# Two products per key tile in place of three: one key head's values stored as high and low parts side by side, and the halves of the result added

## The chip, the cores and the metric

The kernel runs on one core of one Trainium2 chip. The metric is device time in microseconds (us), the median of several runs. In the profile PE is TensorE (PEld is its weight loads), DVE is VectorE, ACT is ScalarE, POOL is GpSimd and SP is the queue that issues the transfers. A product is written as moving data streamed past a stationary operand (the "weights") that is loaded before.

## The reference, cut to what matters

One step of a one-layer encoder: a recurrent group and a sparse attention group side by side, an output projection, and a gated feed-forward part. There are 1024 new frames of one stream (the prompt) and 8 streams of 16 frames with a cache of 512 (the samples). The change touches the attention of the prompt alone:

```
# 8 query heads of width 64 in two groups of 4; each group shares one of 2 key heads (kv = 0, 1)
s = einsum('bthgd,btkhd->bthgk', q, k[sel]) * 64 ** -0.5     # scores, the keys that were not selected are masked
p = softmax(s)
o = einsum('bthgk,btkhd->bthgd', p, v[sel])                   # values: 64 numbers per key and key head
```

Everything is float32. The kernel keeps that accuracy on TensorE by splitting an operand x into a high part (x rounded to the faster fp32r form) and a low part (x minus the high part), and by adding the products high x high, high x low and low x high.

## The kernel before, in words

The rows of the prompt are cut into 8 tiles of 128 frames, a ninth tile holds the samples. The stages follow each other: normalise and project keys, values and index keys (`norm_kv`); index scores; the recurrent group and the queries, with the search for the selected keys beside them; the first half of the output projection; attention, which runs from about 499 to 672 us of the span and is the stage that the change is in; the second half of the output projection with the second normalisation (`out_tile`); the feed-forward part, more than half of the span.

Each engine runs its instructions in an order fixed beforehand. A planner in the kernel (`run`, line 93) steps through generators, four at a time in attention, by its own estimates of each engine's time; a scheduler behind it then places the instructions by estimates too. `ATT_ORDER` (line 415) names the generators: `attn(i, kv)` for query tile i and key head kv, and `sample_attn(b)` for the eight streams, mixed in between the last prompt tiles.

`attn(i, kv)` (line 1372) goes in three steps. First, for each of its 4 query heads, scores for the (i + 1) * 128 keys allowed (`qk`, two matmuls per piece), then one DVE instruction that masks and finds the maximum (tile m), ACT's exp, and POOL's division by the sum. Then, for each tile kt of 128 keys, `flip` transposes the 4 heads' probabilities (4 transposes of 128x128, line 217 of the profile, into one PSUM bank) and `split` writes their high part with ACT and their low part with DVE into one of four buffers `pT` (in the tiles rest and smr). Last, `product(kt)` (line 1431) multiplies them with the values and gathers all key tiles in one PSUM bank, `po`; after the last one ACT copies the 64 rows that belong to this key head to yF (line 1454).

The values are split once, in `norm_kv` (lines 582 and 583, POOL for the high and DVE for the low part) into `vhl`: for each tile a block of 128 columns of high parts (64 for each key head) and a block of 128 columns of low parts. `mm3` (line 245) issues the three matmuls: low values with high probabilities, high with low, high with high. Their output has 128 rows, and the 64 of the other key head are not used. There are 36 pairs of query tile and key tile and two key heads, so 72 products and 216 matmuls of 512 columns.

The lines of helpers in the profile: L207 is any split matmul, L217 a transpose, L1556 the transposes of the samples' probabilities, L66 every instruction of DVE, ACT and POOL.

Of the kernel before, what the change touches and what calls it, by code (L numbers as in the profile page):

```python
# [14 lines left out]
AF = mybir.ActivationFunctionType  # L15
ALU = mybir.AluOpType
# [6 lines left out]
NP = 8  # L23
# [58 lines left out]
class Kernel:  # L82
# [470 lines left out]
    def norm_kv(self, i, tp, g, wk):  # L553
        nc, I, O = self.nc, self.I, self.O
        self.n_norm += 1
        x = self.x.pop(i, None)
        if x is None:
            x = tp.tile([128, D], F32, tag="x", name="x", bufs=4)
            nc.sync.dma_start(x, self.x_src(i))
        if i < len(self.X_T):  # L560
            yield from self.until(self.X_T[i])
        yield from self.norm_T(x, x, g, self.h[i // 3], (i % 3) * 128, tp)
        t = self.ready
        yield 0.0
        yield from self.until(max(t, self.WK_T))
        pk = self.ps()
        for d in range(ND):
            self.mm3(pk[:, :328], self.h_lhs(i, d, 0), self.h_lhs(i, d, 1), wk[:, d, 0, :], wk[:, d, 1, :],
                     d == 0, d == ND - 1)
        self.begin()  # L570
        kv = tp.tile([128, 328], F32, tag="kv", name="kv")
        nc.scalar.activation(kv, pk[:, :328], AF.Copy)
        tab = self.tables(tp, i)
        kr = tp.tile([128, 64], F32, tag="kr", name="kr")
        self.rope(kr[:, None, :], kv[:, None, 256:320], tab, 1, tp, "dve", self.KR_E[i > 2], "dve")
        t = self.end() + self.KV_LAT
        nc.gpsimd.tensor_scalar(self.kn[:, i, :], kv[:, 0:128], 1.0, 0.0, op0=ALU.mult, op1=ALU.add)
        sq = tp.tile([128, 128], F32, tag="sq", name="sq")
        for a in range(2):
            nc.scalar.activation(sq[:, a * 64:a * 64 + 64], kv[:, a * 64:a * 64 + 64], AF.Square, scale=0.125,  # L580
                                 accum_out=self.kss[:, i, a:a + 1])
        self.hi(self.vhl[:, i, 0, :], kv[:, 128:256], "pool")
        self.lo(self.vhl[:, i, 1, :], kv[:, 128:256], self.vhl[:, i, 0, :])
        vo = O["v_p"][0, i * 128:(i + 1) * 128] if i < NP else O["v_s"].rearrange("b t k d -> (b t) k d")
        nc.sync.dma_start(vo.rearrange("t k d -> t (k d)"), kv[:, 128:256])
        nc.gpsimd.tensor_scalar(self.wi[:, i, :], kv[:, 320:328], 8.0 ** -0.5 * 64.0 ** -0.5, 0.0,
                                op0=ALU.mult, op1=ALU.add)
        ko = O["ki_p"][0, i * 128:(i + 1) * 128] if i < NP else O["ki_s"].rearrange("b t d -> (b t) d")
        nc.sync.dma_start(ko, kr)
        yield 0.0  # L590
        yield from self.until(t)
        self.stack_keys(kr, self.ki1[:, i * 128:(i + 1) * 128], self.ki2[:, i * 128:(i + 1) * 128])
# [779 lines left out]
    def attn(self, i, kv, tp):  # L1372
        nc = self.nc
        W = 128 * (i + 1)
        nch = 1 if W <= 512 else 2
        n = W // nch
        mask = self.mask01[:, 256 - W:] if i < 2 else self.s[i]
        while not self.k_done or i not in self.masked or i not in self.q_ok or (kv and i not in self.qst):
            yield 0.5
        if kv == 0:  # L1380
            self.begin()
            self.qst[i] = self.stack_queries(self.qn[:, i, :], 4, self.raw, "raw")
            self.qst_t[i] = self.end()
            yield 0.0
        yield from self.until(self.qst_t[i])
        qe, qo = self.qst[i]
        pb = []
        per = 2 if nch == 1 else 1
        turn = self.m_next
        self.m_next += 1  # L1390
        for j in range(4):
            h = 4 * kv + j
            if j % per == 0:
                while self.wused >= self.SLOTS or self.m_turn != turn:
                    yield 0.5
                self.wused += 1
                ms = self.wr.tile([128, 1024], F32, tag="w", name="m")
            self.begin()
            m = ms[:, 512 * (j % per):]
            mx = tp.tile([128, 4], F32, tag="mx", name="mx", bufs=6)  # L1400

            for c in range(nch):
                sl = slice(c * n, (c + 1) * n)
                pc = self.ps()
                self.qk(pc[:, :n], qe, qo, h, self.k1[:, kv, sl], self.k2[:, kv, sl])
                nc.vector.tensor_tensor_reduce(m[:, sl], pc[:, :n], mask[:, sl], -0.125, mx[:, 0:1] if c else -LOW,
                                               ALU.add, ALU.min, mx[:, c:c + 1])
            t0 = self.chain
            nc.scalar.activation(m[:, :W], m[:, :W], AF.Exp, scale=-1.0, bias=mx[:, nch - 1:nch],
                                 accum_out=mx[:, 3:4])  # L1410
            nc.vector.reciprocal(mx[:, 3:4], mx[:, 3:4])
            nc.gpsimd.tensor_scalar(m[:, :W], m[:, :W], mx[:, 3:4], 0.0, op0=ALU.mult, op1=ALU.add)
            pb.append(m)
            self.m_turn += j == 3
            t = self.end()
            yield 0.0
            yield from self.until(t if j == 3 else t0 - self.AHEAD)
        po = self.ps()
        pTs, ready = {}, {}

        def flip(kt):
            pt = self.ps()
            for j in range(4):
                self.tr(pt[:, j * 128:(j + 1) * 128], pb[j][:, kt * 128:(kt + 1) * 128])
            x = self.pT_free.pop(0)
            pTs[kt] = (x, x.rearrange("p (x n) -> p x n", x=2))
            self.begin()
            self.split(pTs[kt][1], pt)
            ready[kt] = self.end()

        def product(kt):
            x, pT = pTs.pop(kt)
            self.mm3(po, self.vhl[:, kt, 0, :], self.vhl[:, kt, 1, :], pT[:, 0], pT[:, 1], kt == 0, kt == i)
            self.pT_free.append(x)

        for kt in range(i + 1):
            if not self.pT_free and pTs:
                yield from self.until(ready[kt - 1])
                product(kt - 1)
                yield 0.0  # L1440
            while not self.pT_free:
                yield 0.2
            flip(kt)
            if kt == i:
                self.wused -= 4 // per
            yield 0.0
            if kt - 1 in pTs:
                yield from self.until(ready[kt - 1])
                product(kt - 1)
                yield 0.0  # L1450
        yield from self.until(ready[i])
        product(i)
        a = slice(64 * kv, 64 * kv + 64)
        nc.scalar.activation(self.yF[a, :, i * 128:(i + 1) * 128], po[a].rearrange("p (j t) -> p j t", j=4), AF.Copy)

    def sample_prep(self):
        nc = self.nc
# [279 lines left out]
```

## Time and profile before

| | |
|---|---|
| time, median of 3 runs | 1557.31 us (1556.19 to 1558.42) |
| the profiled execution's own time | 1558.3 us |
| its span | 1556.1 us |
| PE busy over the span | 1477.2 us (95%) |
| DVE, ACT, POOL busy | 876.0 (56%), 613.5 (39%), 274.0 us (18%) |

The shares are means over stages with different limits: in the feed-forward part DVE and ACT are idle most of the time, in attention both are nearly as busy as PE. So attention is read by itself below. PE's busy time is modelled with pipelined ends, and a full share says little alone; the chain of waits says whether something else released PE.

### The profile page before, as it was taken

How to read it: one execution, taken by the hardware profiler on the slowest of the kernel's cores; microseconds unless marked ns; L12 is line 12 of the kernel's file. 1: busy time of each engine (PE TensorE's matmuls, PEld its weight loads, DVE VectorE, ACT ScalarE, POOL GpSimd, SP SyncE). 2: the span in 40 equal slices, each digit the busy share in tenths (PEclk: the TensorE clock that was granted, in tenths of full speed). 3: DMA queues.
4: the chain of work that ended last, by engine and by line, in shares of the span. 5: the costliest groups of instructions: out<-in, count | busy, mean ns of one | idle time of the engine just before them, and what ended most of it. 6: DMA issues, size and time to landing. Idle time of an engine off the chain costs nothing.

```text
span 1556.1 us, 20869 instructions
## 1 busy us (share of the span) xinstructions
PE 1477.2 (95%) x7786; PEld 1313.2 (84%) x7786; DVE 876.0 (56%) x1909; ACT 613.5 (39%) x1467; POOL 274.0 (18%) x425
## 2 busy tenths in 40 slices
PE   6889899889869999999999999999999999999998
PEld 6777688778525788889999998989898989898987
DVE  7556899889986988677233333342424242414143
ACT  6447988987203977655202020212021212111100
POOL 4214233334882444300000000000000000000000
PEclk9999899999979999999999999999999999999999
DMA  7201111001400002122102020202020111111003
GB/s 240 57 16 35 42 37 30 14 21 62 163 19 16 1 15 69 28 68 73 64 0 82 0 82 1 82 2 81 16 67 27 55 40 43 49 33 55 28 1 122
DMA packets 95093, 75.24 MB, mean 48 GB/s; under 512 B 13380, under 2 KB 85828, under 8 KB 94992
## 3 DMA queue, kind: packets, MB, share of 16 engines
q1 hardware_dynamic: 94992, 73.91, 15.7%
q8 instruction: 61, 1.00, 0.3%
q14 instruction: 40, 0.33, 0.1%
HBM read 67.62 MB, written 6.27 MB: 47 GB/s over the span
## 4 chain that ended last, share of the span: by engine, by line
PE 74%; DVE 12%; ACT 7%; issue 4%; POOL 1%; DMA 1%; SPq 0%; ACTq 0%; DVEq 0%; POOLq 0%
PE ps L207 67%; DVE junk L66 4%; PE ps L212 4%; PE ps L217 3%; ACT jk L66 3%; DVE tk_cand L66 2%; ACT m L66 1%; ACT L66 1%; DVE s L66 1%; DVE tr L66 1%; ACT tr L66 1%; DVE qn L66 1%; ACT relu L66 1%; POOL qn L66 0%; DMA x<-in_x_prompt_dram 0%
## 5 line engine op out<-in xcount | busy, mean ns | idle before, releaser
L207 PE MATMUL ps<-hf,w 128*128 128x384 f32 x2556 | 460.6, 338 | 0.0
L207 PEld LDWEIGHTS ps<-hf,w 128*128 128x128 f32 x2556 | 451.5, 187 | 0.8
L207 PE MATMUL ps<-w,a 128*128 128x512 f32 x999 | 239.1, 390 | 0.0
L66 DVE TENSOR_TENSOR acc<-ps,acc 128x512 f32<-128x512 f32 x234 | 160.9, 690 | 120.4 <-PE ps L207 119.1
L207 PEld LDWEIGHTS ps<-w,a 128*128 128x128 f32 x999 | 187.4, 188 | 40.1
L66 DVE TENSOR_TENSOR sg<-ps,sg 128x384 f32<-128x384 f32 x66 | 36.8, 557 | 280.2 <-PE ps L207 279.6
L66 ACT ACTIVATE w<-raw 128x512 fp32r<-128x512 f32 x124 | 75.2, 628 | 300.2 <-PE ps L207 220.6
L66 DVE TENSOR_TENSOR w<-raw,w 128x512 fp32r<-128x512 f32 x116 | 76.8, 687 | 85.1 <-ACT w L66 84.9
L66 ACT ACTIVATE a<-sg 128x384 fp32r<-128x384 f32 x66 | 34.5, 523 | 221.2 <-DVE sg L66 221.2
L207 PE MATMUL ps<-hf,rest 128*128 128x384 f32 x612 | 114.5, 334 | 0.0
L66 ACT ACTIVATE jk<-s,tk_cand 128x384 bf16<-128x384 f32 (+3 forms) x128 | 99.4, 776 | 31.9 <-DVE tk_cand L66 29.3
L207 PE MATMUL ps<-h,w 128*128 128x384 f32 x576 | 107.3, 344 | 0.0
L207 PEld LDWEIGHTS ps<-hf,rest 128*128 128x128 f32 x612 | 106.9, 188 | 0.2
L207 PEld LDWEIGHTS ps<-h,w 128*128 128x128 f32 x576 | 101.0, 188 | 3.9 <-ACT relu L66 0.2
L207 PE MATMUL ps<-w,h 128*128 128x256 f32 (+1 forms) x600 | 95.5, 314 | 0.0
L207 PEld LDWEIGHTS ps<-w,h 128*128 128x128 f32 x600 | 82.8, 188 | 6.6
L66 ACT ACTIVATE sg<-ps 128x384 f32<-128x384 f32 x66 | 32.0, 485 | 121.9 <-PE ps L207 121.9
L212 PE MATMUL ps<-wa,yF 128*128 128x512 f32 x144 | 67.7, 626 | 3.1 <-DVE acc L66 2.2
L212 PEld LDWEIGHTS ps<-wa,yF 128*128 128x128 f32 x144 | 28.2, 202 | 38.5 <-issue 32.8
L66 POOL TENSOR_SCALAR m<-m,mx 128x128 f32<-128x128 f32 (+7 forms) x64 | 47.4, 748 | 64.7 <-DVE mx L66 57.3
L207 PE MATMUL ps<-smr,vhl 128*128 128x512 f32 x162 | 54.0, 419 | 1.3 <-ACT smr L66 1.1
L66 DVE TENSOR_TENSOR a<-sg,a 128x384 fp32r<-128x384 f32 x66 | 36.8, 557 | 32.6 <-ACT a L66 32.6
(261 smaller groups left out, 2163.7 us busy)
## 6 DMA issues: line engine op xcount, KB each, us to landing
raw<-in_w_ffn_in_dram SPq DMA_DIRECT2D x44, 512.0 KB, 4.7
raw<-in_w_ffn_out_dram SPq DMA_DIRECT2D x22, 512.0 KB, 3.6
raw<-in_w_in_dram SPq DMA_DIRECT2D x16, 512.0 KB, 5.0
out_dram<-acc SPq DMA_DIRECT2D x9, 512.0 KB, 2.6
x<-in_x_prompt_dram SPq DMA_DIRECT2D x8, 512.0 KB
acc<-in_x_prompt_dram SPq DMA_DIRECT2D x8, 512.0 KB
tab<-in_rope_dram SPq DMA_DIRECT2D x43, 64.0 KB, 1.7
wa<-in_w_out_dram SPq DMA_DIRECT2D x4, 512.0 KB
```

Source lines behind the costliest of these rows:

```text
L66: return f(*args, **kw)
L207: self.nc.tensor.matmul(out, lhsT, rhs, start=start, stop=stop)
L212: self.nc.tensor.matmul(out, lhsT, rhs, start=start, stop=stop)
L217: self.nc.tensor.transpose(out, in_, self.ident[0:n, 0:n])
```

## The change

In a prompt tile's `vhl` the columns are ordered anew: block 0 holds key head 0 as 64 high and 64 low columns, block 1 the same for key head 1. The stationary operand of a product is now one block of one key head. It is multiplied with the probabilities' high parts and then with their low parts, both times into `po`. Rows 0 to 63 of `po` then hold high values times both parts, rows 64 to 127 low values times both parts (low x low is now in the sum too), and the two halves are added: ACT copies one half to yF, and a new DVE instruction adds the other half from PSUM. The samples' tile keeps the old layout and its three matmuls.

```diff
-        self.hi(self.vhl[:, i, 0, :], kv[:, 128:256], "pool")
-        self.lo(self.vhl[:, i, 1, :], kv[:, 128:256], self.vhl[:, i, 0, :])
+
+        v, vs = self.vhl[:, i], kv[:, 128:256]
+        if i < NP:
+            v = v.rearrange("p a (x d) -> p x a d", x=2)
+            vs = vs.rearrange("p (a d) -> p a d", a=2)
+        self.hi(v[:, 0], vs, "pool")
+        self.lo(v[:, 1], vs, v[:, 0])
...
         def product(kt):
             x, pT = pTs.pop(kt)
-            self.mm3(po, self.vhl[:, kt, 0, :], self.vhl[:, kt, 1, :], pT[:, 0], pT[:, 1], kt == 0, kt == i)
+            for q in range(2):
+                self.mm(po, self.vhl[:, kt, kv], pT[:, q], kt == 0 and q == 0, kt == i and q == 1)
             self.pT_free.append(x)
...
         product(i)
-        a = slice(64 * kv, 64 * kv + 64)
-        nc.scalar.activation(self.yF[a, :, i * 128:(i + 1) * 128], po[a].rearrange("p (j t) -> p j t", j=4), AF.Copy)
+
+        a, b = (slice(64 * x, 64 * x + 64) for x in (kv, 1 - kv))
+        y = self.yF[a, :, i * 128:(i + 1) * 128]
+        nc.scalar.activation(y, po[b].rearrange("p (j t) -> p j t", j=4), AF.Copy)
+        nc.vector.tensor_tensor(y, po[a].rearrange("p (j t) -> p j t", j=4), y, op=ALU.add)
```

Up to attention no engine's instructions move. Within it the planner and the scheduler set another order, shown at three places.

DVE, early in attention, around the end of the first two tiles; m,mx is the mask and maximum of one head, smr and rest the low parts of the probabilities, qeo the queries. Before:

```order
L66 TENSOR_TENSOR smr<-ps,smr 128x512 [waits Activation_49]
L66 TENSOR_TENSOR qeo<-ps,qeo 64x512 [waits Activation_49]
L66 TENSOR_TENSOR qeo<-ps,qeo 64x512
L66 ISA m,mx<-ps,kn 128x256 [waits PE_49,Pool_49]
L66 ISA mx 128x1
L66 ISA m,mx<-ps,kn 128x256 [waits PE_49,Pool_49]
L66 ISA mx 128x1
L66 RECIPROCAL mx<-mx 128x1 [waits Activation_49]
L66 TENSOR_TENSOR smr<-ps,smr 128x512 [waits Activation_49]
```

The same place in the changed kernel:

```order
L66 TENSOR_TENSOR qeo<-ps,qeo 64x512
L66 TENSOR_TENSOR yF<-ps,yF 64x4x128 [waits Activation_49]
L66 ISA m,mx<-ps,kn 128x256 [waits PE_49,Pool_49]
L66 ISA mx 128x1
L66 ISA m,mx<-ps,kn 128x256 [waits PE_49,Pool_49]
L66 ISA mx 128x1
L66 RECIPROCAL mx<-mx 128x1 [waits Activation_49]
L66 ISA m,mx<-ps,s_888 128x384 [waits PE_49,Pool_49]
L66 ISA mx 128x1
L66 TENSOR_TENSOR smr<-ps,smr 128x512 [waits Activation_49] x2
L66 TENSOR_TENSOR yF<-ps,yF 64x4x128 [waits Activation_49]
```

The two additions stand in DVE's queue ahead of the masks of the heads that follow, and each waits for ACT's copy.

PE, late in attention, among the products of tile 7; vhl marks a product's matmuls, ident,m the transposes of the probabilities, k and qeo the scores. Before:

```order
L207 MATMUL ps<-smr,vhl 128x512 x2
L217 MATMUL ps<-ident,m 128x128 x4
L207 MATMUL ps<-rest,vhl 128x512 x3
L207 MATMUL ps<-smr,vhl 128x512
L217 MATMUL ps<-ident,m 128x128 x12
L207 MATMUL ps<-smr,vhl 128x512 x5
```

and changed:

```order
L207 MATMUL ps<-k_4342,qeo 128x512
L217 MATMUL ps<-ident,m 128x128 x4
L207 MATMUL ps<-rest,vhl 128x512 x2
L217 MATMUL ps<-ident,m 128x128 x12
L207 MATMUL ps<-smr,vhl 128x512 x3
L1565 MATMUL ps<-ident,kn 128x128 x5
```

The runs of three and more matmuls of a product have become runs of two and three, with the same transposes between.

PE, near the end of attention, from the last scores of one sample (ksT) to the transposes of its probabilities (L1556 before, L1565 now). Before:

```order
L207 MATMUL ps<-ksT,rest 128x16 x3
L217 MATMUL ps<-ident,m 128x128 x2
L217 MATMUL ps<-ident,smp 128x128 x4
L217 MATMUL ps<-ident,m 128x128 x2
L1556 MATMUL ps<-ident,smp 128x128 x5
```

and changed:

```order
L217 MATMUL ps<-ident,smp 128x128 x4
L207 MATMUL ps<-smr,rest 128x264 x2
L207 MATMUL ps<-smr,rest 128x248 x2
L207 MATMUL ps<-ksT,rest 128x16 x3
L217 MATMUL ps<-ident,m 128x128 x2
L1565 MATMUL ps<-ident,smp 128x128 x5
```

Eight transposes stood between the two before, and two stand there now; the rest moved ahead of the scores.

## Rows read from the trace of the kernel before

**Rows 1.** Five stretches: length, busy PE, PEld, DVE, ACT, POOL; granted clock, DMA
```profile
499.00:517.00 18.00, 15.66 (x85) 13.61 (x86) 16.20 (x74) 17.15 (x53) 7.82 (x19) 0.83 0.00 1
517.00:555.00 38.00, 36.88 (x224) 31.23 (x223) 33.23 (x102) 32.95 (x74) 15.22 (x22) 1.00 0.00 1
555.00:578.00 23.00, 21.19 (x126) 18.22 (x124) 20.38 (x66) 17.63 (x38) 10.84 (x13) 1.00 0.08 24
578.00:646.00 68.00, 67.81 (x464) 60.44 (x464) 53.70 (x147) 51.59 (x127) 34.26 (x40) 1.00 0.21 55
646.00:672.00 26.00, 22.93 (x131) 19.49 (x131) 15.19 (x31) 14.61 (x38) 1.60 (x2) 0.93 0.23 49
```

**Rows 2.** The chain of waits by line and tile, for the first four of these stretches
```profile
by line: ACT m L66 46.9%; ACT qeo L66 13.2%; ACT yF L66 9.9%; ACT smr L66 8.0%; ACT rest L66 6.0%; DVE rest L66 3.9%; DVE qeo L66 3.9%; PE ps L207 3.7%; DVE m L66 3.2%; issue 3.0%; DVE mx L66 0.2%
...
by line: PE ps L207 66.9%; PE ps L217 28.2%; ACT smr L66 1.6%; ACT yF L66 1.5%; ACT rest L66 1.3%; ACT m L66 0.5%; issue 0.4%
...
by line: issue 25.2%; DVE m L66 19.8%; ACT m L66 14.8%; DVE smr L66 10.2%; ACT smr L66 5.2%; ACT smp L66 3.9%; DVE mx L66 3.9%; PE ps L207 3.6%; DVE qeo L66 3.2%; DVE w L66 3.1%; ACT qeo L66 2.6%; DVE rest L66 2.6%; ACT w L66 2.1%; ACT rest
...
by line: PE ps L207 72.2%; PE ps L217 23.1%; PE ps L1556 4.2%; DVE w L66 1.0%; issue 0.2%; ACT smr L66 0.1%; ACTq L66 0.0%
```

**Rows 3.** The chain of waits, 593 to 598 us: start, duration, what
```profile
594.10 0.69 PE ps L207 x3
...
596.56 0.44 PE ps L217 x4
```

**Rows 4.** The same stretches, matmuls and loads on the tile of values: PE, PEld
```profile
499.00:517.00 18.00, 4.92 (x13) 2.20 (x13) 0.00 (x0) 0.00 (x0) 0.83 0.00 1
517.00:555.00 38.00, 21.14 (x66) 11.07 (x66) 0.00 (x0) 0.00 (x0) 1.00 0.00 1
555.00:578.00 23.00, 9.87 (x31) 5.18 (x29) 0.00 (x0) 0.00 (x0) 1.00 0.08 24
578.00:646.00 68.00, 29.36 (x102) 17.42 (x102) 0.00 (x0) 0.00 (x0) 1.00 0.21 55
646.00:672.00 26.00, 9.50 (x30) 5.38 (x30) 0.00 (x0) 0.00 (x0) 0.93 0.23 49
```

**Rows 5.** The samples' matmuls on the same tile, 578 to 646 us
```profile
L207 PE MATMUL ps<-pTn,vhl 128*128 128x128 f32 x18 | 3.3, 274 | 0.0
```

**Rows 6.** Instructions on the tile of stacked queries: durations (ns) smallest, median, largest
```profile
L207 PEld LDWEIGHTS ps<-k,qeo x192: 186/188/337, 497.4 to 638.7; 128*128 128x128 f32 x192
...
L66 ACT ACTIVATE qeo<-ps x28: 588/592/599, 91.2 to 606.1; 64x512 fp32r<-64x512 f32 x28
L66 DVE TENSOR_TENSOR qeo<-ps,qeo x28: 682/689/696, 92.4 to 607.4; 64x512 fp32r<-64x512 f32 x28
```

**Rows 7.** Splitting the values: durations (ns), first and last start
```profile
L66 POOL TENSOR_SCALAR vhl<-kv x9: 291/299/349, 23.9 to 72.3; 128x128 fp32r<-128x128 f32 x9
L66 DVE TENSOR_TENSOR vhl<-kv,vhl x9: 273/291/308, 26.9 to 72.7; 128x128 fp32r<-128x128 f32 x9
```

**Rows 8.** ACT's copies of finished tiles, one row for each stretch: busy, mean, idle before
```profile
L66 ACT ACTIVATE yF<-ps 64x512 f32<-64x512 f32 x3 | 1.8, 594 | 0.1
L66 ACT ACTIVATE yF<-ps 64x512 f32<-64x512 f32 x6 | 3.6, 592 | 0.6 <-PE ps L207 0.5
L66 ACT ACTIVATE yF<-ps 64x512 f32<-64x512 f32 x1 | 0.6, 591 | 0.0
L66 ACT ACTIVATE yF<-ps 64x512 f32<-64x512 f32 x5 | 2.9, 586 | 1.0 <-PE ps L207 1.0
L66 ACT ACTIVATE yF<-ps 64x512 f32<-64x512 f32 x1 | 0.6, 596 | 0.0
```

**Rows 9.** Ten microseconds in which three engines were dense
```profile
540.00:550.00 10.00, 10.00 (x67) 8.90 (x67) 9.65 (x31) 8.97 (x20) 3.96 (x5) 1.00 0.00 0
```

**Rows 10.** PE in order of time, 645 to 649 us
```profile
644.75 0.40 PE L207 MATMUL ps<-ksT,rest 128*128 128x16 f32 x3
...
649.15 0.48 PE L1556 MATMUL ps<-ident,smp 128*128 128x128 f32 x1 [3.06 <-POOL smp L66]
```

## The prediction, made before the changed kernel ran

> **What bounds the kernel now.** I began with the busy table by stretch, to see which engines are dense together in attention, and cut attention where the picture changes [rows 1]. In the first stretch (499 to 517) ACT is busy 17.15 of 18 us and DVE 16.20; in the second (517 to 555) PE 36.9 of 38, DVE 33.2, ACT 33.0; in the third (555 to 578) DVE 20.4 of 23; in the fourth (578 to 646) PE 67.8 of 68, DVE 53.7, ACT 51.6; the fifth (646 to 672) has holes on all engines. As PE's busy time includes modelled ends, I took the chain of waits next, for each stretch [rows 2]. The reader is to see that it is not PE throughout: in the first stretch the chain lies on ACT (its exps 47%, its copies of finished tiles 9.9%), in the second 95% on PE's split matmuls and transposes, in the third on DVE, ACT and issue, in the fourth 99% on PE. So PE time taken away is worth its full price in the fourth stretch alone, something in the second, and little in the first and third. Behind attention everything is a later stage in the same order, which moves with it.
>
> **What is removed.** One matmul of 512 columns for each product. What one costs on the chain: three stand there for 0.69 us, so 0.23 us each [rows 3]. By that the 72 removed ones are 16.6 us of PE. Where they are: the matmuls on the values by stretch are 13, 66, 31, 102 and 30 [rows 4], of which 18 in the fourth are the samples' [rows 5] and, at three for each sample, 6 in the fifth. A third of the rest goes: 4.3, 22 and 10.3 products in the first three stretches (8.4 us together), 28 in the fourth (6.4 us), 8 in the fifth (1.8 us). The weight loads that go with them lie beside the matmuls and give nothing of their own. The second matmul of a product has the same stationary block as the first, yet I expect it to be loaded again: the scores too use one block twice in a row, and 192 loads stand there, one for each matmul, at 188 ns [rows 6].
>
> [...]
>
> **What is added.** 16 DVE additions of 64x512 from PSUM and SBUF. The nearest row is the queries' subtraction, 64x512 from PSUM and SBUF, at 0.689 us [rows 6]; that is 11.0 us. By the copies that they follow [rows 8], 3, 6, 1, 5 and 1 of them fall into the five stretches. ACT's copies stay 16; each now reads one half of the partitions and writes the other, as ACT's queries do at 0.592 against 0.59 now [rows 6, 8], so 0. An addition waits for ACT's copy, which waits for the last product; behind it in DVE's queue stand masks and maxima of the heads that follow (the first place of the order), on which exp, division, transposes and PE hang in turn. Bounds for one addition: 0 where DVE would have idled, 0.69 + 0.59 = 1.28 where the copy's and its own time both lie on the chain. One of eight PSUM banks is also held 0.7 us longer; as the planner puts the additions behind work that is ready, I take 0 for it, and the upper bound above contains it.
>
> **What is moved early.** The split of the values takes the same elements in two runs of 64; 9 instructions on POOL at 0.30 and 9 on DVE at 0.29, done by 73 us [rows 7], while the first product comes after 500. Cover enough: 0; were the form twice as slow and uncovered, 8 x 0.59 = 4.7 us, which I leave out as no row speaks for it.
>
> **The sum by stretch.** First to third, 79 us: DVE has 69.8 us of work [rows 1] and gets 10 x 0.689, so 76.7; ACT stays at 67.7, PE loses 8.4. DVE becomes the bound. How densely it can work while ACT and PE are dense too is seen at 540 to 550: 9.65 of 10 [rows 9]. 76.7 / 0.965 = 79.5, that is 0.5 us more than now: the removed PE time buys nothing here, since the engine that was behind PE gets the new work. The ends: DVE without any gap, 76.7 (2.3 less); DVE at its share of now, 69.8 / 79 = 88%, 86.8 (7.8 more). I take the row's share, since it is the densest that all three engines hold together.
>
> Fourth, 68 us: PE 67.8 less 6.4 is 61.4, DVE 53.7 plus 5 x 0.689 is 57.1. PE stays the bound, but DVE then has 93% and there is less product work to stand in for the samples' waits. What that gives back I take from the fifth stretch, where the order can be compared: between a sample's last scores and the transposes of its probabilities PE waits 3.06 us for POOL [rows 10], after eight transposes of other heads that now are two (the third place of the order); a transpose is 0.11 us [rows 3], so 6 x 0.11 = 0.66 of 1.84 us comes back, 35%. The same share of 6.4 is 2.2: the stretch gets 4.2 us shorter. The ends: 6.4, and 0 (five additions at 1.28).
>
> Fifth: 1.84 less 0.66, 1.2 us shorter (ends 1.8 and 0). [...]
>
> Sum: 0.5 - 4.2 - 1.2 = 4.9 us less. The profiled execution took 1558.3 us, 2.2 around its span of 1556.1; 1553.4 by its own time, and as it is 1.0 above the median, 1552.4 for the median.
>
> **The rivals.**
> (a) The relief is swallowed. DVE reaches 93% in the first three stretches (82.5 us, 3.5 more), and in the fourth two thirds of the 6.4 come back as waits of the samples (2.1 less), with 1.2 less at the end: 0.2 more, 1557.5. For it: DVE is at 88% already and two engines are on the chain there; against it: the fourth stretch's chain, 99% PE.
> (b) Slower: the additions stop DVE's queue. Each holds what is behind it until ACT has copied; DVE keeps its 88% in the first three stretches, 7.8 more, the fourth gains nothing, the fifth 1.2: 6.6 more, 1563.9. It decides from the point where DVE is busy under 91% of the first three stretches (84.4 us, 5.4 more, which eats 4.2 and 1.2). For it: the copies are 9.9% of the first stretch's chain [rows 2]. Against it: ACT itself has stood before such a copy for 0.1, 0.6, 0, 1.0 and 0 us in all [rows 8], so the planner places work that follows a product when it is ready.
> [...]
> (c) Larger gain: DVE without gaps (2.3 less), the fourth and fifth stretch in full (6.4 and 1.8): 10.5 less, 1546.8. For it: 9.65 of 10 shows that DVE can be dense. Against it: over 79 us at once no engine is.
> (d) A removed matmul frees only half of its step, as the two that remain run against their loads (0.188 each): 28 x 0.115 less 2.2 in the fourth, 8 x 0.115 less 0.66 in the fifth, 0.5 more before: 0.8 less, 1556.5. Against it: the 0.69 for three.
> [...]
>
> **How the numbers follow.** Forecast 0.54, (a) 0.18, (b) 0.17, (c) 0.08, (d) 0.03. A measurement of this kernel tells 0.2% from no change, 3.1 us, so faster is under 1554.2 and slower over 1560.4. The forecast's own range is 1549.5 to 1556, a fifth of it above 1554.2: faster 0.43 + 0.08 = 0.51; same 0.11 + 0.17 + 0.03 = 0.31; slower 0.17 and 0.01 of (a), 0.18. The range 1548 to 1561 leaves out most of (b) and of (c), under 0.2.
>
> **What would show it.** Products: 144 matmuls of 512 columns on the values, still 0.23 us each on the chain, 144 loads. Additions: 16 at 0.69. The first three stretches, up to the copy of query tile 5's first key head near 578, as long as now within 2 us, with DVE near 96% and the chain moved from PE to DVE; the fourth about 4 us shorter with PE still on the chain; a wait for POOL near 3.7 us ahead of the late sample's transposes. The prediction is wrong if the first part grows by over 5 us, if the chain of the fourth leaves PE, or if PE's waits for the samples take back the whole 6.4 us.

## The result, and the profile of the changed kernel

The changed kernel is slower: 1571.99 us median (1569.03 to 1573.52), against 1557.82 us for the kernel before (1556.19 to 1558.42) on the same chip, ratio 1.009 with a 95% interval of 1.0072 to 1.0109. The prediction was 1552.4 us. Its profiled execution took 1570.77 us, its span is 1568.9 us.

To compare the traces I cut them at five events that both have: the start of the last matmul of the output projection's first half (before attention), ACT's copies of query tile 5, key head 0, of tile 7, key head 0, and of tile 7, key head 1 (the last), and the first activation of the feed-forward part (tile sg). Lengths between them, in us:

| kernel | up to copy (5,0) | to copy (7,0) | to the last copy | out stage, to the feed-forward | sum |
|---|---|---|---|---|---|
| before | 84.9 | 63.9 | 28.9 | 63.5 | 241.2 |
| changed | 88.9 | 65.7 | 29.1 | 73.1 | 256.8 |
| difference | +4.0 | +1.8 | +0.2 | +9.6 | +15.6 |
| forecast | +0.5 | -4.2 | -1.2 | 0 | -4.9 |

The feed-forward part is 0.7 us shorter and attention began 2.1 us earlier, which makes 12.8 of span. The 2.1 us are not the change's doing: no instruction ahead of attention has moved, and over all the kernels run here, whatever they change, the first event lies between 491.1 and 494.2 us. The five stretches by busy time, in the changed kernel (columns as in [rows 1]):

```profile
499.00:517.00 18.00, 15.98 (x78) 11.51 (x78) 16.21 (x69) 17.11 (x54) 7.85 (x19) 0.89 0.00 1
517.00:555.00 38.00, 32.64 (x193) 25.96 (x192) 35.69 (x107) 31.75 (x70) 15.83 (x23) 1.00 0.00 1
555.00:578.00 23.00, 19.15 (x103) 15.93 (x100) 18.91 (x60) 16.15 (x34) 8.30 (x9) 0.85 0.08 24
578.00:646.00 68.00, 62.52 (x423) 55.31 (x421) 56.38 (x155) 51.75 (x124) 33.11 (x40) 0.97 0.18 48
646.00:672.00 26.00, 20.94 (x135) 18.36 (x135) 15.49 (x36) 14.02 (x38) 4.28 (x5) 0.87 0.12 33
```

PE has fewer matmuls in the first four stretches, and it is busy for less time in each but the first (15.98 us against 15.66). But DVE's share of the first 79 us is 70.81, 90%, against 69.81 (88%) in [rows 1]: it got additions and hardly became denser. The chain of waits of the second and the fourth stretch, to be laid beside [rows 2]:

```profile
by line: PE ps L207 29.5%; DVE m L66 14.2%; PE ps L217 12.4%; issue 10.3%; ACT m L66 8.2%; DVE qeo L66 7.3%; DVE smr L66 4.5%; ACT smr L66 3.9%; ACT yF L66 3.1%; DVE mx L66 2.1%; ACT rest L66 1.6%; DVE rest L66 1.6%; DVE yF L66 1.1%; DVEq L
...
by line: PE ps L207 41.5%; PE ps L217 20.1%; DVE m L66 9.4%; PE ps L1565 5.5%; issue 4.9%; DVE smp L66 3.7%; DVE smr L66 2.4%; POOL smp L66 2.4%; ACT m L66 2.3%; DVE rest L66 1.9%; ACT smr L66 1.6%; POOL kn L66 1.2%; DVE yF L66 1.0%; DVE w 
```

In the fourth stretch the chain was 99% PE; now PE has 67% of it (41.5, 20.1 and 5.5), the rest is DVE, ACT, POOL and issue. The new work itself has the size that was forecast: 144 matmuls, each with its load, and 16 additions.

```profile
L207 PEld LDWEIGHTS ps<-smr,vhl x106: 186/189/337, 505.2 to 672.8; 128*128 128x128 f32 x106
...
L207 PEld LDWEIGHTS ps<-rest,vhl x38: 186/188/337, 503.2 to 666.4; 128*128 128x128 f32 x38
...
L66 DVE TENSOR_TENSOR yF<-ps,yF x16: 673/689/695, 507.8 to 676.6; 64x512 f32<-64x512 f32 x16
```

The largest part of the loss lies behind attention. The chain of waits there (start, duration, what):

```profile
669.74 4.21 DMA raw<-in_w_out_dram
...
674.72 8.07 PE ps L207 x34
...
682.82 1.22 DVE acc L66 x2
684.04 0.68 DVE rest L66
684.72 0.14 issue
684.85 3.01 PE ps L207 x12
687.86 2.12 issue
689.98 1.38 PE ps L217 x8
```

PE waits for a transfer of w_out, then for DVE's sum and split, then for the issue of transposes. By four microseconds (columns as above), PE has holes from 680 to 692, and the mean granted clock of the last two rows is 0.82 and 0.75 (in steps of one microsecond 1.00 up to 690 us, 0.50 from 691 to 694 us and 1.00 from there):

```profile
680.00:684.00 4.00, 3.25 (x15) 2.32 (x13) 1.18 (x2) 1.18 (x3) 0.00 (x0) 1.00 0.46 125
684.00:688.00 4.00, 2.99 (x12) 2.17 (x12) 1.82 (x8) 3.81 (x7) 0.00 (x0) 1.00 0.00 0
688.00:692.00 4.00, 2.02 (x10) 1.87 (x11) 4.00 (x11) 1.19 (x2) 0.00 (x0) 0.82 0.00 0
692.00:696.00 4.00, 4.00 (x15) 3.24 (x14) 1.44 (x3) 0.57 (x1) 0.00 (x0) 0.75 0.00 0
```

In the kernel before, whose last copy comes 3.9 us earlier, PE is all but full in the same part of the stage and the granted clock stays at 1.00:

```profile
676.00:680.00 4.00, 3.84 (x17) 3.08 (x17) 2.05 (x7) 3.94 (x8) 0.00 (x0) 1.00 0.31 121
680.00:684.00 4.00, 4.00 (x20) 3.26 (x19) 3.90 (x11) 0.88 (x2) 0.00 (x0) 1.00 0.02 4
684.00:688.00 4.00, 4.00 (x27) 3.55 (x26) 3.57 (x9) 3.32 (x7) 0.00 (x0) 1.00 0.00 0
```

### The profile page after: what moved, and what is told of

The parts are those of the page before. It is cut to its first block, busy times and chain, and to the rows that moved or that the text cites. A ratio compares the mean times of both kernels' runs of the same rounds, so it can differ in the third digit from the quotient of the medians.

```text
span 1568.9 us, 20754 instructions
## 1 busy us (share of the span) xinstructions
PE 1474.0 (94%) x7714; PEld 1304.6 (83%) x7714; DVE 884.7 (56%) x1925; ACT 614.3 (39%) x1467; POOL 273.9 (17%) x425
## 4 chain that ended last, share of the span: by engine, by line
PE 65%; DVE 5%; issue 2%; ACT 1%; POOL 1%; DMA 0%; POOLq 0%; DVEq 0%; ACTq 0%; SPq 0%
PE ps L207 59%; PE ps L212 2%; PE ps L217 2%; DVE m L66 1%; POOL qn L66 0%; ACT m L66 0%; DVE smr L66 0%; DVE qn L66 0%; PE ps L1565 0%; DVE qeo L66 0%; DVE ps L66 0%; DVE smp L66 0%; DMA raw<-in_w_out_dram 0%; ACT smr L66 0%; POOL kn L66 0%
## 5 line engine op out<-in xcount | busy, mean ns | idle before, releaser
L66 ACT ACTIVATE jk<-s,tk_cand 128x384 bf16<-128x384 f32 (+3 forms) x128 | 99.4, 777 | 31.7 <-DVE tk_cand L66 29.1
L212 PEld LDWEIGHTS ps<-wa,yF 128*128 128x128 f32 x144 | 28.5, 205 | 38.8 <-issue 33.3
L207 PE MATMUL ps<-w,rest 128*128 128x512 f32 x216 | 54.0, 404 | 2.9 <-DVE rest L66 1.6
```

The lines of the kernel that those rows point to most:

```text
L66: return f(*args, **kw)
L207: self.nc.tensor.matmul(out, lhsT, rhs, start=start, stop=stop)
L212: self.nc.tensor.matmul(out, lhsT, rhs, start=start, stop=stop)
```

## The experiments

Two theories: the work (the additions on DVE cost more than the removed matmuls give), or the order (the planner and the scheduler, with other estimates to go by, set an order that is worse, whatever the work).

### One half of the change alone

Two products without the additions (half of the sum is missing: the high parts of the values for key head 0, the low parts for key head 1):

```diff
-        nc.vector.tensor_tensor(y, po[a].rearrange("p (j t) -> p j t", j=4), y, op=ALU.add)
```

> Two products as in the changed kernel, the 16 additions left out (so the low parts of the values are missing from the result). Theory 1 (DVE work: the additions sit on the engine that ends much of attention, and eat the saved PE time): attention, from the last matmul on wa,yF to the last copy to yF, falls from 177.7 us before and 183.7 changed to 168 to 173, the time to 1545 to 1553. Theory 2 (order: the new order of the instructions, above all at the passage from attention to the second output projection, costs the time, whatever the work): attention 175 to 184, and the stage behind it, from there to the first gated copy (sg), between 63 and 74 us as the order falls out; the time 1552 to 1570.

Measured: 1565.03 us, ratio 1.0047 [1.0032, 1.0062].

Three products as before, and the additions (which add the wanted half once more, so that the result is doubled; the work on DVE is that of the change):

```diff
+        y = self.yF[a, :, i * 128:(i + 1) * 128]
...
+        nc.vector.tensor_tensor(y, po[a].rearrange("p (j t) -> p j t", j=4), y, op=ALU.add)
```

> The kernel before with its three products, and 16 additions of the same shape behind the copies (the result is added to itself). Theory 1: 16 x 0.69 us of DVE without any PE time saved: attention 184 to 190 us, time 1564 to 1572. Theory 2: the additions alone cost at most half of their 11 us in attention (178 to 183), and the stage behind is 63 to 74 as the order falls out.

Measured: 1567.42 us, 1.0063 [1.0048, 1.0078]. A kernel that only leaves out 72 matmuls is slower than before: the work alone can't explain that. Its out stage takes 72.4 us, that of the second 63.8. The second fits the work theory: its attention takes 187.9 us, within 184 to 190 and over the order theory's 178 to 183. In the first, attention takes 177.2 us, hardly less than the 177.7 before and within the order theory's 175 to 184; the work theory wanted 168 to 173.

### The planner's estimates

The changed work, planned as if it were the old (the third matmul is still counted, the addition is not: issued through `nc.nc` it bypasses the planner's account):

```diff
+            self.pe += 512 / 2400.0
...
-        nc.vector.tensor_tensor(y, po[a]...
+        nc.nc.vector.tensor_tensor(y, po[a]...
```

> The changed kernel, but the planner in the kernel keeps the accounts of before: the third matmul's time is still charged to PE and the addition is not charged to DVE, so that the generators are stepped as before (the scheduler behind it still sees the true instructions). Theory 1: the same work, so 1565 to 1575. Theory 2: with the order of before most of the loss goes: the stage behind attention 63 to 66 us, time 1553 to 1561.

Measured: 1563.18 us, 1.003 [1.0018, 1.0041], between the ranges of the two theories; its out stage takes 65.5 us, as the order theory said.

The old work, planned as if it were the new:

```diff
+            self.pe -= 512 / 2400.0
...
+        k, t = self, self.now()
+        k.fill("vector", t)
+        k.busy["vector"] = max(k.busy["vector"], t) + 0.07 + 512 * 0.00104
```

> The kernel before with the planner's accounts of the changed one: a third matmul that costs PE nothing, and an addition charged to DVE that isn't issued. Theory 1: the work of before, 1555 to 1561. Theory 2: the planner's order of the changed kernel, 1563 to 1575, the stage behind attention over 68 us.

Measured: 1569.21 us, 1.007 [1.0054, 1.0087], as the order theory said, with an out stage of 69.1 us. The estimates alone cost 11 us with the work unchanged. But in these four the scheduler still moves instructions by the work itself, so each has an order of its own. The next four don't.

### Work and order apart

Every instruction is tied behind the one that stands before it on its engine in a given order (an edge of order alone, with no wait on a semaphore). The order is that of the kernel before, or of the changed one, on all five engines; removed matmuls drop out of it, an addition stands one DVE instruction behind its copy.

```diff
+    def pin(self):
...
+                    tc.add_manual_dep(mine[e][at], last.name, dep, reason="pin")
```

> The changed kernel's whole work (two products, 16 additions), with every engine's instructions tied to the order that they have in the kernel before; each addition stands one DVE instruction behind the place of the copy that it needs. Order theory (the new order costs the time, the work does not): the loss of 14 us goes, and what is left is the gain that I had forecast for the work, 1549 to 1556 us; out stage 63 to 65 us as before. Work theory (the additions and the waits they bring cost the time, in any order): still slower, 1563 to 1572.

> Two products, the 16 additions left out (half of the sum is missing in the result), tied to the order of the kernel before. Both theories: faster than before, as PE has 72 matmuls less. Order theory: 1547 to 1553, against 1565 for the same work in the order that it got by itself. If it is not under 1556, the removed matmuls are worth nothing even in the old order, and a third reason is needed.

> Three products as before, with 16 additions (a half that is not used is added, so the result is off), tied to the order of the kernel before. Order theory: the additions by themselves cost at most 16 x 0.69 = 11 us and some of it lies beside PE, 1558 to 1565, against 1567 for the same work in its own order. Work theory: 1567 or more, as the additions hold up what stands behind them whatever the order.

> The work of the kernel before (three products, no additions), tied to the order of the changed kernel on every engine; the third matmul of a product stands right behind the second. Order theory: the loss is here without the change's work, 1567 to 1574, attention near 184 us and the out stage near 70 or more. Work theory: within 3 us of the kernel before, 1555 to 1561.

Measured, beside 1557.75 us for the kernel before (15 runs):

| work | order | us | ratio, interval | up to (5,0) | to (7,0) | to the last copy | out stage |
|---|---|---|---|---|---|---|---|
| two products, additions | old | 1562.20 | 1.0025 [1.0014, 1.0036] | 89.9 | 65.2 | 28.5 | 64.2 |
| two products | old | 1554.16 | 0.9976 [0.9965, 0.9986] | 84.4 | 62.4 | 28.5 | 62.5 |
| three products, additions | old | 1565.08 | 1.0045 [1.0031, 1.0059] | 90.7 | 65.4 | 30.1 | 64.5 |
| three products (as before) | new | 1577.94 | 1.0126 [1.0112, 1.0140] | 90.6 | 69.6 | 28.5 | 71.2 |

Both theories hold a part. In the old order the new work costs 4.5 us: the products give 3.6, and the additions take 7.3 alone and 8.0 beside the two products. For the same new work the order costs 9.8 us (1571.99 less 1562.20). For the old work it costs 20.2, and in the new order the new work is 5.9 us faster than the old (1571.99 against 1577.94). So the two costs do not simply add: the new order suits the new work better than the old. The first row lies between the order theory's 1549 to 1556 and the work theory's 1563 to 1572, the second is faster than before but not by as much as the order theory said (1547 to 1553), the third is at the upper end of its 1558 to 1565, and the fourth went beyond its 1567 to 1574. By stage, attention is 6 us longer with the new work in either order (183.6 and 183.7 us in all, against 177.7), and 11 us longer with the old work in the new order (188.7); the out stage keeps its 63 to 65 us in the old order whatever the work, and takes over 71 in the new.

Why do the products give so little? The chain of the fourth stretch, in two products without additions:

```profile
by line: PE ps L207 33.9%; issue 11.0%; PE ps L217 9.7%; DVE m L66 6.9%; ACT m L66 6.4%; PE ps L1583 5.7%; ACT smr L66 4.3%; DVE smr L66 3.5%; DVE rest L66 3.0%; POOL smp L66 2.4%; ACT rest L66 2.3%; ACT smp L66 1.9%; ACT kn L66 1.9%; DVE s
```

PE falls from 99% to about half (33.9, 9.7 and 5.7), with the stretch only 1.5 us shorter by the copies: close behind PE's path stood another over DVE, ACT and POOL. (These rows are of 578 to 646 us; by the copies the stretch ends at 639.4 here, and up to there PE's share is half as well.)

### What of an addition costs: its wait or its length

Both in the old order with the new work. In the first the additions, but for the last, stand four DVE instructions later. In the second they cover one of four heads (three quarters of the other half are missing):

```diff
-        nc.nc.vector.tensor_tensor(y, po[a].rearrange("p (j t) -> p j t", j=4), y, op=ALU.add)
+        nc.nc.vector.tensor_tensor(y[:, 0:1], po[a].rearrange("p (j t) -> p j t", j=4)[:, 0:1], y[:, 0:1], op=ALU.add)
```

> As the new work in the old order, but each addition (except the last) stands four DVE instructions later in DVE's queue, so that ACT's copy is long done when DVE comes to it. If the additions cost by stopping the queue (2.5 us of waits for the copy in five of them), attention gets 2 us or more shorter than 183.6 and the time goes to 1560 or below. If they cost by DVE's own time, attention stays within 1.5 us of 183.6 and the time within 2 us of 1562.2.

> As the new work in the old order, but each addition covers 128 of its 512 columns (three quarters of the other half are missing in the result), at the same places with the same waits. If the additions cost DVE's own time, their price falls with their length (0.69 to about 0.25 us, so by 60 to 70 percent of the 8 us between 1562.2 and 1554.2): 1556 to 1558. If they cost the wait and the place in the queue, 1560 to 1562.

Measured: 1561.88 us for the late ones (1.0023 [1.0015, 1.0032]), 1556.78 for the short ones (0.9985 [0.9976, 0.9994]). On the tile yF the trace of the new work in the old order names, as what DVE and others sat idle for (us, times),

```profile
  PE ps L207: 9.7, 6
  ACT yF L66: 2.5, 5
  ACT rest L66: 0.4, 1
```

and with the late additions

```profile
  PE ps L207: 9.3, 5
  ACT rest L66: 0.4, 1
```

The wait for ACT's copies is gone, and the time is the same within the spread. The late additions also keep the PSUM bank of a finished tile for longer, 4.0 us on average from the start of ACT's copy to the end of the addition, against 1.97 in the old order without the delay: that is not what costs either. The short additions are 0.289 us in place of 0.688:

```profile
L1482 DVE TENSOR_TENSOR yF<-ps,yF x16: 276/289/296, 508.7 to 671.8; 64x128 f32<-64x128 f32 x16
```

That is 16 times 0.40, 6.4 us of DVE less, and the time falls by 5.4 (6.2 by the two ratios, 0.0040 of the time). So an addition costs by DVE's own time, and of the time cut here nearly all shows; the wait that it brings costs nothing that can be measured. (Of the additions in full, 11.0 us, 7.3 to 8.0 showed.)

### The first two tiles of the out stage

The order of PE at the end of attention, kernel before (tile 0 gathers in ps_6808 and tile 1 in ps_6825; smr,vhl are attention's last products):

```
L207 MATMUL ps_6808<-w_6708,rest_4026 128x512 x2
L207 MATMUL ps_6808<-w_6714,rest_4026 128x512
L207 MATMUL ps_6825<-w_6708,rest_4026 128x512 x2
L207 MATMUL ps_6740<-pTn_4694,vhl_87 128x128 x2
L207 MATMUL ps_6575<-smr_4171,vhl_87 128x512
L207 MATMUL ps_6825<-w_6714,rest_4026 128x512
```

and changed, where tile 0 (ps_6755, its second half ps_6773) goes first alone and tile 1 (ps_6789) follows after attention's last product:

```
L207 MATMUL ps_6755<-w_6682,rest_4026 128x512 x2
L207 MATMUL ps_6755<-w_6703,rest_4026 128x512 x3
L207 MATMUL ps_6526<-smr_4171,vhl_87 128x512
L207 MATMUL ps_6773<-w_6711,rest_4026 128x512
L207 MATMUL ps_6789<-w_6655,rest_4026 128x512 x3
```

Before, 22 matmuls of the out stage stand ahead of attention's last product; now 12. The third tile's split of yF needs one of the two buffers in rest that the first two tiles hold, so it comes after tile 0's second half, which waits for the second transfer of w_out: that is the chain shown above (DMA, 34 matmuls, acc, rest). Of the kernels so far, those with the tiles side by side (the kernel before, three products with additions, the changed work with the old estimates) have out stages of 63.5, 63.8 and 65.5 us, those one by one (changed, two products without additions, the old work with the new estimates) 73.1, 72.4 and 69.1. Two small rules test it. In the changed kernel:

```diff
+            if q and i < 2:
+                self.half_a += 1
+                while self.half_a < 2:
+                    yield 0.2
```

> The changed kernel, with one rule more in the out stage: tile 0 begins its second half only when tile 1 has begun its first, so the first two tiles use each block of weights side by side, as in the kernel before; attention's order is that of the changed kernel. If the out stage's 9.6 us come from those two tiles going one after the other: out stage 64 to 66 us in place of 73, attention 184 as in the changed kernel, 1561 to 1565 us. If they come from how attention ends (the late sample, the transfers of w_out), the out stage stays over 70 and the time at 1569 or more.

and the reverse in the kernel before:

```diff
+            if not i and q:
+                self.half_a = 1
+            while i == 1 and not q and not self.half_a:
+                yield 0.2
```

> The reverse: the kernel before, unchanged but that tile 1 of the out stage waits with its first half until tile 0 begins its second, as the changed kernel has it. If the one-after-the-other is the cause: out stage 69 to 73 us in place of 63.5, attention 178 as before, 1563 to 1568 us. If not: within 3 us of the kernel before.

The reverse came out nearly as expected: 1562.89 us, 1.0025 [1.0016, 1.0035], the out stage 68.9 us in place of 63.5, attention 178.4. The old kernel now has the changed one's hole and the lower clock behind it, four microseconds each:

```profile
676.00:680.00 4.00, 3.32 (x14) 2.18 (x12) 2.17 (x6) 3.97 (x7) 0.00 (x0) 1.00 0.00 0
680.00:684.00 4.00, 2.06 (x10) 1.99 (x11) 3.78 (x10) 1.37 (x4) 0.00 (x0) 0.79 0.00 0
684.00:688.00 4.00, 4.00 (x15) 3.21 (x15) 1.94 (x4) 0.79 (x2) 0.00 (x0) 0.79 0.02 4
```

The first missed: 1569.61 us, 1.0075 [1.0061, 1.0089], only 2.4 less than the changed kernel. Its out stage did fall, to 65.8 us, but up to the last copy it takes 189.7 us in place of 183.7, 6.0 more. Of these, 2.7 lie behind the copy (7,0): 24 matmuls of the out stage now stand ahead of attention's last product in place of 12, and twelve are 2.8 us at the 0.23 of [rows 3]. The other 3.3 lie ahead of the copy (7,0), where the order is the changed kernel's; 1.6 of them come at one place, between the copies (5,1) and (6,0). Here it is, at a hole of 1.92 us that PE has in both executions,

```profile
592.00:596.00 4.00, 2.46 (x14) 2.27 (x15) 2.65 (x10) 3.05 (x7) 2.95 (x4) 0.86 0.01 2
596.00:600.00 4.00, 4.00 (x25) 3.86 (x24) 2.48 (x8) 2.11 (x4) 0.19 (x1) 0.72 0.00 0
```

and in the changed kernel

```profile
592.00:596.00 4.00, 2.74 (x20) 2.62 (x21) 2.65 (x10) 3.09 (x7) 2.95 (x4) 1.00 0.01 2
596.00:600.00 4.00, 4.00 (x34) 3.75 (x32) 3.86 (x11) 3.32 (x9) 2.08 (x3) 1.00 0.06 17
```

the same hole, with the clock at 0.72 behind it in the one (in steps of half a microsecond 0.50 from 595 to 597.5 us; over 600 to 604 us it is 1.00 again) and at 1.00 in the other. Where the remaining 1.7 us come from, and whether the executions without a trace have this too, is not shown. So the order of the two tiles is worth 2.4 us by taking it out of the changed kernel and 4.3 by putting it into the old one (medians, 1562.89 less 1558.62 for the kernel before beside it). That leaves much of the order's 9.8 us. By stage, the changed kernel and the new work in the old order have the same attention (183.7 and 183.6 us) and differ in the out stage (73.1 and 64.2). But ten matmuls of the out stage, 2.3 us, have changed places there: in the old order they stand ahead of attention's last product (22 against 12). So about 2.3 of these 8.9 us belong to attention, which without them is longer in the new order. At its end PE waits 4.3 us for POOL in one piece (the other two rows are the holes of the out stage),

```profile
PE ps L1565 <- POOL smp L66: 4.3, 1, 4.3
PE ps L217 <- issue: 2.1, 1, 2.1
PE ps L207 <- DVE rest L66: 1.6, 1, 1.6
```

against 3.06 in [rows 10]. How the rest divides I have not settled.

## Why the prediction was wrong

By the first table the forecast missed 3.5 us in the first three stretches, 6.0 in the fourth, 1.4 in the fifth and 9.6 behind attention, where it had counted nothing.

- **Products: the terms were right, their worth was not.** 144 matmuls with 144 loads, as forecast, and next to no gain in the first three stretches (0.5 us in the old order). In the fourth I took 6.4 less 2.2. Alone the products gave 1.5 us there in the old order, and 0.1 in the order that they got by themselves (63.8 against 63.9). The step that failed is "PE stays the bound": a chain that is 99% PE says which path ends last, not how far behind the next one is. By the run in the old order the next was about 1.5 us behind, of 64.
- **Additions: this was the larger error in attention.** I divided DVE's work by 0.965, the share of its densest ten microseconds [rows 9], and got 0.5 us. In the old order the new work costs 5.0 us there, in the changed kernel 4.0, with DVE at 91% and 90%. Its row for the new work in the old order:

```profile
499.00:578.00 79.00, 68.04 (x373) 53.14 (x374) 71.67 (x236) 64.25 (x158) 32.17 (x50) 0.96 0.03 8
```

For the 5.0 the other end that I had put down, DVE at its share of now (7.8), was the nearer one; the 4.0 are nearest to rival (a)'s 3.5. In the fourth stretch I priced the additions at nothing; they cost 1.5 us of it alone (65.4 against 63.9) and 2.8 beside the two products (65.2 against 62.4).
- **Rival (b) had nearly the right size and the wrong reason.** It gave 6.6 us more; in the old order the new work takes 6.6 us more from attention to the feed-forward part (4.5 in the time). That the sums agree is luck: its terms were 7.8, 0 and -1.2, and measured were 5.0, 1.3 and -0.4, with 0.7 in the out stage. And it is not the held queue that costs: without the wait nothing changed, with shorter additions most of the cost went. The trace of the new work in the old order does show such waits for ACT's copies, 2.5 us in five pieces; but taking these waits away was worth nothing that can be measured (1561.88 us against 1562.20).
- **"Behind attention everything is a later stage in the same order, which moves with it" was false.** This step alone missed 9.6 us (some 2.3 of them are the ten matmuls that moved out of attention). The order of the out stage had changed too, and the two tiles one after the other could be read in the order before the run. I looked at three places of attention and at none behind it.
- **The late sample** was forecast right in direction: the wait for POOL grew from 3.06 to 4.3 us (I had 3.7). The stretch around it did not get 1.2 us shorter but 0.2 longer; with the two products alone in the old order it got 0.4 shorter. Its second price, the clock behind the hole, I had left out. Changed, from 652 to 660 us:

```profile
652.00:656.00 4.00, 1.53 (x6) 1.46 (x7) 0.60 (x3) 1.38 (x7) 0.80 (x1) 0.63 0.00 0
656.00:660.00 4.00, 4.00 (x18) 3.31 (x16) 1.64 (x4) 1.64 (x4) 0.00 (x0) 0.52 0.00 0
```

and before, from 648 to 656 us, where the second row is back at 0.99:

```profile
648.00:652.00 4.00, 2.85 (x11) 2.37 (x12) 2.30 (x5) 1.48 (x4) 0.80 (x1) 0.58 0.00 0
652.00:656.00 4.00, 4.00 (x34) 3.77 (x32) 2.87 (x6) 1.19 (x2) 0.00 (x0) 0.99 0.00 0
```


Between the theories: the loss of some 14 us is 4.5 for the work in the old order and 9.8 for the order with the new work, shown by runs of the same work in both orders; taken the other way round it is 20.2 for the order with the old work, and the new work then gives 5.9 back. Of the order's part, the first two tiles made 2.4 us when taken out of the changed kernel and 4.3 when put into the old one. No version of this change beat the kernel before by more than 0.24%, the mark of two products without any addition, which does not compute the sum.

## What to carry to other kernels

When a kernel's order is set by estimates, a change of the estimates is a change of every stage behind it: compare the order up to the end, and run the new work tied to the old order before judging either. In the first 79 us of this attention PE, DVE and ACT, which feed each other, were busy for 93, 88 and 86% of the time. In such a place price new work on the second-busiest engine at most of its length (here 7.3 to 8.0 of 11.0 us over all of attention), and removed work on the busiest at no more than the lead over the next path. A share of the chain of waits is no measure of that lead; taking the work away by itself is.

## What the runs showed of the hardware

The granted clock after a hole of PE is not the same in every execution of the same order: with the same hole of 1.92 us at 591 to 594 us, it was 1.00 from 596 to 600 us in one execution and 0.72 in another, and the stretch around it took 1.6 us longer there. And of the 11.0 us that 16 additions keep DVE busy, 7.3 to 8.0 show in the time of a kernel in which PE is busy 94 to 95%.
